# Attention stages of a two-model transformer kernel: three more engines in program order, and a new order of work

## The chip, the core and the metric

The kernel runs on one core of one Trainium2 chip. The core has five engines with instruction streams of their own: TensorE (PE in the profile; PEld is its weight load), VectorE (DVE), ScalarE (ACT), GpSimd (POOL) and SyncE (SP), which issues most DMA transfers. Engines meet through semaphores: an instruction waits on its engine until the instructions that it depends on are done, and what stands behind it on that engine waits too. The metric is the time of one execution on the device, in microseconds (us).

## The reference

Two stacks of two layers each run one after the other on one sequence of 256 tokens, model width 1024, in float32.

```python
# first stack, per layer
x = x + 0.5 * swiglu(rms_norm(x, norm_ffn1), w_ffn1_gate, w_ffn1_up, w_ffn1_down)   # hidden 2816
x = x + mixer(rms_norm(x, norm_mix))        # nsa (8 heads) beside moba (8 heads), then w_out
x = x + 0.5 * swiglu(rms_norm(x, norm_ffn2), ...)
# inside the nsa half of the mixer
kc = gelu(flat(k_cmp + pos_ck) @ w_ck1) @ w_ck2      # w_ck1: 2048 x 256; vc likewise with w_cv1
o = g0 * attend(q, kc, vc) + g1 * selected_blocks(rope(q), ...) + g2 * window(rope(q), ...)
# second stack, per layer (hybrid)
proj = rms_norm(x) @ w_in                   # aq ak av | index q k w | bq bk bv | gates
score = sum_h iw_h * relu(iq_h . ik);  keep the 64 best keys of each query
ya = attention(rope(norm(aq)), rope(norm(ak)), av) over the kept keys         # 8 heads
yb = (softmax(b1) - lam * softmax(b2)) @ bv, normed                           # 4 heads
x = x + (g_a * (ya @ w_up_a) + g_b * (yb @ w_up_b)) @ w_out
x = x + swiglu(rms_norm(x), ...)            # hidden 2816
```

## The kernel before

There are ten stages, in this order: feed-forward, mixer, feed-forward (twice, the first stack), then hybrid, feed-forward (twice, the second). All 256 tokens stay in SBUF, and every stage streams its weights from HBM. A weight chunk of 1 MB is loaded by SP into a buffer `raw` (three buffers of that name; a load waits until the chunk before it in its buffer has been used up). ACT copies the chunk into `hi` in TensorE's reduced float32 format (line 188), and DVE subtracts to get the rest, `lo` (line 189), each in two halves. PE then multiplies three times, with `hi` and `lo` (lines 209 to 211 for a projection). There are four buffers each of `hi` and `lo`.

In the attention stages, PE's own order is written out by hand (`tc.manual_schedule(engines={ENG.PE})`); the other engines' instructions are put in order by the scheduler of the framework. Work for PE comes in two kinds. A list of items, the class `Fill`, holds the large projections of the stage; each is a generator that yields after every few matmuls, and `fill.us(2.5)` runs the next matmuls of the list for about 2.5 us of PE's time, `fill.until("q")` runs the list until the item `q` is done. Between these calls stand the small steps that depend on other engines: transposes (`heads_T`, line 412), scores (line 430), the turning of the exponentials (`p_T`: `P` is transposed on PE and copied to `PT` by ACT, line 455, and DVE, line 458), values (line 486).

The weights of an item are asked for, and split, in one go when the item before it starts (`fetch(i + 1)`).

In the mixer, `blocks` turns the keys and values for the compression, `comp` multiplies them with `w_ck1` and `w_cv1` (line 788). These two matrices come in two halves of 1 MB each through the same `raw` buffers, unsplit: `ck`, `cv` for half 0, `ck'`, `cv'` for half 1. Behind them come a gelu (`z`), and a small product (line 819).

In the hybrid stage, `heads(name)` squares and sums a projection (ACT line 1020, DVE line 1023), takes the power -1/2 on POOL (`hr`, line 203) and applies the rope, `rope_full`: POOL multiplies with the cosine (line 966) and adds (line 976), DVE multiplies with the sine (lines 967 and 970) and with `hr` (line 981). The four projections `xa`, `xk` (sparse half) and `xb`, `xc` (difference half) go through this, then are transposed into `aqT`, `akT`, `bqT`, `bkT` (line 418 is DVE's copy). The index rope is all on DVE, makes `ix` and `ikd`; PE transposes these and DVE copies the result to `iT` (line 1081), from which line 1096 makes the index scores. The choice of the 64 best is 8 pairs of a maximum-of-eight and a replacement (lines 1123 and 1124) for each of two query blocks.

`pipeline` then runs over slots (12 in a mixer, 8 in a hybrid stage): at slot n it issues the scores of slot n + 1, fills, turns slot n, fills, multiplies slot n with its values, fills. `attend` makes such a slot; its coefficient multiplies `P` on DVE (line 471) and, for the last third, on POOL (line 472).

Of the kernel before, what the change touches and what calls it, by code (L numbers as in the profile page):

```python
# [16 lines left out]
ENG = mybir.EngineType  # L17
PSUM = bass.MemoryType.PSUM
# [3 lines left out]
D = 1024  # L22
# [4 lines left out]
NEG = -1e30  # L27
# [6 lines left out]
class K:  # L34
# [196 lines left out]
    def to_residual(self, yh, yl, w, nk, scale, after, held=2, fill=False):  # L231
# [27 lines left out]
        def fetch(c):  # L259
            src = w(c) if callable(w) else w[c * 256 : (c + 1) * 256, :].rearrange("(j p) n -> p j n", p=128)  # L260
            return self.weights(src, [2, D])
# [19 lines left out]
        if fill:  # L281
            return [(None, lambda c=c: fetch(c), lambda hl, c=c: run(c, hl), None) for c in range(nch)], end
        for c in range(nch):
            for _ in run(c, fetch(c)):
                pass
# [3 lines left out]
    def ffn(self, pr, wg, wu, wd, scale, after, start=None, load=None, extra=None):  # L289
# [3 lines left out]
        with tc.tile_pool(name="ffn", bufs=2) as fp:  # L293
# [33 lines left out]
            for c in range((NF + 3) // 4):  # L327
# [25 lines left out]
                if extra is not None and c == 2:  # L353
                    with tc.high_priority(150):
                        extra()
# [5 lines left out]
    def proj_item(self, name, w, c0, n, pr, done):  # L361


        def fetch():
            return [
                self.weights(
                    w[h * 512 : (h + 1) * 512, c0 : c0 + n].rearrange("(k p) f -> p k f", p=128), [4, n]
                )
                for h in range(2)
            ]  # L370
# [15 lines left out]
        return name, fetch, run, None  # L386
# [59 lines left out]
    def p_T(self, pool, p, n, k1):  # L446
# [9 lines left out]
        for i in range(n):  # L456
            nc.tensor.transpose(k1[:, 128 * i : 128 * i + 128], p[:, i, 128:256], self.ident)
        nc.vector.tensor_copy(pt[:, :, 256:384], k1[:, 0 : 128 * n].rearrange("p (i q) -> p i q", i=n))
        return pt

    def attend(self, pool, qk, vs, mask, coef, bank, end, start=True, stop=True):
# [5 lines left out]
        def scores():  # L467
            p, sm = self.scores_exp(pool, qk(), mask)
# [6 lines left out]
            st["p"] = p  # L475

        def turn():
            st["o"] = bank()

            st["pt"] = self.p_T(pool, st["p"], 2, st["o"][:, 256:512] if start else self.acc())  # L480
# [10 lines left out]
        return scores, turn, values  # L491

    def pipeline(self, fill, slots, post, a, b, c):


        slots[0][0]()
        fill.us(3.5)
        for n, (_, turn, values) in enumerate(slots):
            if n + 1 < len(slots):
                slots[n + 1][0]()  # L500
            fill.us(a)
            turn()
            fill.us(b)
            values()
            if n in post:
                post[n]()
            fill.us(c)
# [18 lines left out]
    def mixer(self, l, pr, after):  # L526
# [3 lines left out]
        with tc.tile_pool(name="mix", bufs=1) as mp, ExitStack() as es:  # L530
# [22 lines left out]
            es.enter_context(tc.manual_schedule(engines={ENG.PE}))  # L553
# [99 lines left out]
            def out_rows(c):  # L653
# [19 lines left out]

            rope2(kv[:, :, 256:384])
            next(blocks)
            fill.us(3.0)
# [4 lines left out]
            fill.us(4.0)  # L681
            next(comp)
            fill.us(1.5)
# [5 lines left out]
            fill.us(1.0)  # L689
# [8 lines left out]
            next(comp)  # L698
            fill.us(1.5)
            next(comp)  # L700
            next(comp)
            fill.us(1.0)
            next(comp)
            fill.us(1.2)
            self.heads_T(qrT, q, 0, self.psT, 0.125)
            fill.us(1.2)
            next(comp, None)
            fill.us(0.5)
            self.heads_T(qrT, q, 1, self.psO, 0.125)
            fill.us(0.3)  # L710
            probs = self.cmp_probs(mp, cp, qT, kcb, gt, tok)
            fill.us(1.5)
# [5 lines left out]
                1: lambda: self.heads_T(mq, tok["mq"], 0, self.psT, 0.125),  # L718
                2: lambda: self.heads_T(mq, tok["mq"], 1, self.psT, 0.125),
                5: lambda: self.heads_T(mk, tok["mk"], 0, self.psT),  # L720
                6: lambda: self.heads_T(mk, tok["mk"], 1, self.psT),
# [43 lines left out]
    def compress(self, mp, l, flats, kcb, vcb):  # L765
# [17 lines left out]
        for h in range(2):  # L783
            for i, w in enumerate(ws):
# [9 lines left out]
                if h == 0 and i == 1:  # L794
                    ws = fetch(1)
# [811 lines left out]
```

## Time and profile before

| what | us |
| --- | --- |
| median of 3 runs | 1923.4 (1920.32 to 1925.4) |
| the profiled execution: its time | 1922.36 |
| the profiled execution: its span | 1920.7 |
| PE busy (matmuls) | 1824.2, 95% of the span |
| DVE busy | 1312.5, 68% |
| ACT busy | 1000.1, 52% |
| POOL busy | 618.9, 32% |

The span runs from the first to the last instruction of the profile; the time has 1.7 us around it. All times of day below are microseconds from the span's start. A row of a timeline gives start, length, engine, line, operation, out<-in, and in brackets the idle time before it with what ended it. Matmuls are pipelined, so their lengths overlap.

### The profile page before, as it was taken

How to read it: one execution, taken by the hardware profiler on the slowest of the kernel's cores; microseconds unless marked ns; L12 is line 12 of the kernel's file. 1: busy time of each engine (PE TensorE's matmuls, PEld its weight loads, DVE VectorE, ACT ScalarE, POOL GpSimd, SP SyncE). 2: the span in 40 equal slices, each digit the busy share in tenths (PEclk: the TensorE clock that was granted, in tenths of full speed). 3: DMA queues.
4: the chain of work that ended last, by engine and by line, in shares of the span. 5: the costliest groups of instructions: out<-in, count | busy, mean ns of one | idle time of the engine just before them, and what ended most of it. 6: DMA issues, size and time to landing. Idle time of an engine off the chain costs nothing.

```text
span 1920.7 us, 27216 instructions
## 1 busy us (share of the span) xinstructions
PE 1824.2 (95%) x10136; PEld 1521.3 (79%) x10136; DVE 1312.5 (68%) x2170; ACT 1000.1 (52%) x1948; POOL 618.9 (32%) x660
## 2 busy tenths in 40 slices
PE   8899989999999999899999987899999897999999
PEld 7788866788788878667887776798888786888887
DVE  6766567776677665677766587767765787667763
ACT  6554445655555454456555544545554544546552
POOL 6451112254225411112542254012441442014540
PEclk9999999999999999999999998999999998999999
DMA  7547462354655464623546534245546444255543
GB/s 241 193 134 242 158 192 91 112 186 146 239 173 186 144 241 147 206 88 112 183 147 232 177 110 153 89 153 176 181 149 228 151 132 153 89 176 175 170 168 123
DMA packets 149077, 314.42 MB, mean 164 GB/s; under 512 B 5588, under 2 KB 30320, under 8 KB 148944
## 3 DMA queue, kind: packets, MB, share of 16 engines
q1 hardware_dynamic: 148016, 311.15, 49.4%
q0 software_dynamic: 896, 1.52, 0.4%
q8 instruction: 80, 1.31, 0.3%
q14 instruction: 53, 0.43, 0.1%
q10 hardware_dynamic: 32, 0.01, 0.0%
HBM read 311.61 MB, written 1.05 MB: 163 GB/s over the span
## 4 chain that ended last, share of the span: by engine, by line
PE 62%; DVE 17%; POOL 9%; ACT 7%; issue 4%; DMA 1%; SPq 0%; ACTq 0%; POOLq 0%; DVEq 0%
DVE lo L189 9%; PE acc L310 8%; PE acc L252 8%; PE acc L251 8%; PE acc L256 8%; PE acc L314 4%; PE acc L209 3%; PE psS L310 3%; ACT hi L188 3%; PE acc L210 3%; PE acc L211 3%; POOL hh L351 2%; POOL g L339 2%; ACT P L441 2%; PE psT L310 2%
## 5 line engine op out<-in xcount | busy, mean ns | idle before, releaser
L189 DVE TENSOR_TENSOR lo<-raw,hi 128x1024 fp32r<-128x1024 f32 (+1 forms) x604 | 745.3, 1258 | 206.7 <-ACT hi L188 202.3
L188 ACT ACTIVATE hi<-raw 128x1024 fp32r<-128x1024 f32 (+1 forms) x604 | 590.3, 1009 | 197.2 <-PE acc L256 110.8
L310 PE MATMUL acc<-xx,hi 128*128 128x512 f32 x1056 | 371.8, 397 | 8.0 <-DVE gcol L138 7.4
L314 PE MATMUL acc<-xx,lo 128*128 128x256 f32 x1056 | 291.4, 279 | 0.0
L310 PEld LDWEIGHTS acc<-xx,hi 128*128 128x128 f32 x1056 | 198.6, 189 | 53.0 <-DVE gcol L138 7.7
L252 PE MATMUL acc<-lo,gh 128*128 128x512 f32 x528 | 209.9, 397 | 3.8 <-DVE lo L189 3.8
L251 PE MATMUL acc<-hi,gh 128*128 128x512 f32 x528 | 209.4, 397 | 0.0
L314 PEld LDWEIGHTS acc<-xx,lo 128*128 128x128 f32 x1056 | 199.7, 189 | 1.8
L339 POOL TENSOR_TENSOR g<-g,rbc 128x256 f32<-128x256 f32 x132 | 136.4, 1046 | 175.1 <-DVE g L324 121.3
L310 PE MATMUL psS<-xx,hi 128*128 128x512 f32 x528 | 190.7, 395 | 2.1 <-ACT hi L188 2.1
L351 POOL TENSOR_TENSOR hh<-g,u 128x256 f32<-128x256 f32 x132 | 139.6, 1065 | 162.2 <-DVE u L324 162.2
L256 PE MATMUL acc<-hi,gl 128*128 128x512 f32 x528 | 173.7, 395 | 0.0
L209 PE MATMUL acc<-hi,xx 128*128 128x512 f32 (+2 forms) x416 | 171.2, 412 | 0.2 <-ACT xx L1462 0.2
L211 PE MATMUL acc<-hi,xx 128*128 128x512 f32 (+2 forms) x416 | 161.8, 389 | 1.1 <-DVE xx L1463 1.0
L210 PE MATMUL acc<-lo,xx 128*128 128x512 f32 (+2 forms) x416 | 161.5, 389 | 0.0
L349 POOL TENSOR_TENSOR g<-g,rbc 128x256 f32<-128x256 f32 x132 | 134.8, 1027 | 65.4 <-DVE g L342 65.4
L222 ACT ACTIVATE gh<-hh 128x256 fp32r<-128x256 f32 x132 | 55.2, 418 | 180.8 <-POOL hh L351 180.3
L314 PE MATMUL psS<-xx,lo 128*128 128x256 f32 x528 | 147.3, 279 | 1.1 <-DVE lo L189 1.1
L341 ACT ACTIVATE th<-g 128x256 f32<-128x256 f32 x132 | 55.0, 417 | 153.0 <-POOL g L339 152.6
L342 DVE SCALAR_TENSOR_TENSOR g<-th,g 128x256 f32<-128x256 f32 x132 | 83.4, 635 | 73.2 <-ACT th L341 73.2
L252 PEld LDWEIGHTS acc<-lo,gh 128*128 128x128 f32 x528 | 99.1, 188 | 28.6 <-DVE lo L189 5.4
L223 DVE TENSOR_TENSOR gl<-hh,gh 128x256 fp32r<-128x256 f32 x132 | 57.7, 437 | 92.2 <-ACT gh L222 92.2
(429 smaller groups left out, 3486.9 us busy)
## 6 DMA issues: line engine op xcount, KB each, us to landing
raw<-in_w_in_dram SPq DMA_DIRECT2D x60, 1024.0 KB, 5.1
raw<-in_w_ffn_down_dram SPq DMA_DIRECT2D x44, 1024.0 KB, 5.0
raw<-in_w_ffn_up_dram SPq DMA_DIRECT2D x40, 1024.0 KB, 5.1
raw<-in_w_ffn_in_dram SPq DMA_DIRECT2D x40, 1024.0 KB, 5.2
raw<-in_w_ffn_gate_dram SPq DMA_DIRECT2D x39, 1024.0 KB, 5.1
raw<-in_w_ffn_out_dram SPq DMA_DIRECT2D x22, 1024.0 KB, 5.0
raw<-in_w_out_dram SPq DMA_DIRECT2D x12, 1024.0 KB, 4.9
raw<-in_w_ffn_gate_dram SPq DMA_DIRECT2D x10, 512.0 KB, 3.8
```

The costliest lines, as they stand in the source:

```text
L188: nc.scalar.activation(hi[:, hs], raw[:, hs], AF.Copy),
L189: nc.vector.tensor_tensor(lo[:, hs], raw[:, hs], hi[:, hs].bitcast(F32), op=ALU.subtract),
L209: mm(out, ah, bh, start=start, stop=False)
L210: mm(out, ah, bl, start=False, stop=False)
L211: self.last = mm(out, al, bh, start=False, stop=stop)
L251: mm(accs[t, n], ah, hi[:, j, cs], start=k == 0, stop=False)
L252: mm(accs[t, n], ah, lo[:, j, cs], start=False, stop=False)
L256: mm(accs[t, n], al, hi[:, j, cs], start=False, stop=k == nk - 1)
L310: nc.tensor.matmul(banks[j], hi[:, k, fs], xk.rearrange("p u s -> p (u s)"), start=h == 0 and k == 0, stop=False,)
L314: self.last = nc.tensor.matmul(banks[j][:, 0:S], lo[:, k, fs], xk[:, 0, :], start=False, stop=h == 1 and k == 3,)
L339: nc.gpsimd.tensor_tensor(g, g, pr.rbc, op=ALU.mult)
L351: nc.gpsimd.tensor_tensor(hh, sgs[j], u, op=ALU.mult)
```

## The change

DVE, ACT and POOL are also taken out of the scheduler's hands inside the mixer and hybrid stages, so the order of their instructions there is now the order of the code. The code is laid out for it:

- The halves of a weight chunk are objects (`Chunk`): while an item of the list runs, the halves of the next item are split one by one, evenly over the item's steps. Before a half is split, the chunks of the next six halves (three chunks) are asked for, that is, their DMA is issued on SP. The list's first item is split before the stage's own code starts (`prime`).
- `fill.later(t, f)` puts a step off until `t` us of filled PE time have gone by. The rope's products, sum and norm, the squares' sums, and the top-k pairs (one each 1.5 us) are such steps.
- Hybrid: the items come in the order xb, xc, gate, xa, xk (before: xa, xk, gate, xb, xc); each pair of transposes moves along.
- `pipeline` keeps scores two slots ahead, and the coefficient's product is a step of its own (`weigh`) a fill later. The last third of `P` is multiplied on DVE instead of POOL.
- `comp`: `ck` and `cv` are taken in turn, so that both must have landed from its start; 16 matmul rows stand in one block where two blocks of 8 stood with fill between them.

```diff
+MANUAL = {ENG.PE, ENG.Activation, ENG.DVE, ENG.Pool}
...
-            es.enter_context(tc.manual_schedule(engines={ENG.PE}))
...
+            fill.prime()
+            es.enter_context(tc.manual_schedule(engines=MANUAL))
...
+class Chunk:
+    def ask(self):
+        if self.raw is None:
+            self.raw = self.k.wraw(self.src, self.shape)
+    def half(self, h):
...
+        nc.scalar.activation(self.hi[:, hs], self.raw[:, hs], AF.Copy)
+        nc.vector.tensor_tensor(self.lo[:, hs], self.raw[:, hs], self.hi[:, hs].bitcast(F32), op=ALU.subtract)
...
+    def split(self, upto):
+        while self.pos < min(upto, len(self.halves)):
+            for c, _ in self.halves[self.pos : self.pos + 6]:
+                c.ask()
+            c, h = self.halves[self.pos]
+            c.half(h)
+            self.pos += 1
...
+            if self.i + 1 < len(self.items):
+                a, b = self.upto[self.i + 1 : self.i + 3]
+                self.split(a + int((b - a) * min(1.0, self.n / steps)))
+            self.tick(t)
```

The compression and the mixer's calls around it:

```diff
         for h in range(2):
-            for i, w in enumerate(ws):
-                for j in range(0, 8, 2):
+            for j in range(0, 8, 2):
+                for i, w in enumerate(ws):
...
-                if h == 0 and i == 1:
-                    ws = fetch(1)
-                yield
+            if h == 0:
+                ws = fetch(1)
+            yield
...
             next(comp)
-            fill.us(4.0)
-            next(comp)
-            fill.us(1.5)
+            fill.us(4.5)
             next(comp)
             fill.until("q")
```

The slots, and the hybrid's rope and order:

```diff
-            nc.gpsimd.tensor_tensor(
+            nc.vector.tensor_tensor(
                 p[:, :, 256:384], p[:, :, 256:384], c[:, 2:4, None].to_broadcast([128, 2, 128]), op=ALU.mult
             )
...
+        for n in range(2):
+            slots[n][0]()
+            fill.tick(0.85)
+            fill.us(2.2)
+            slots[n][1]()
...
+            if n + 2 < len(slots):
+                slots[n + 2][0]()
...
+                    fill.later(3.2, root)
                     for t in range(2):
-                        self.rope_full(
+                        steps = self.rope_full(
...
+                        for d, f in zip(((1.2, 2.8, 6.8), (3.6, 5.2, 8.0))[t], steps):
+                            fill.later(d, f)
...
+            index_top(1.5)
             fill.until("xc")
-            fill.us(5.0)
+            fill.us(1.0)
             self.heads_T(bqT, tok["xb"], 0, self.psT, 0.125)
             self.heads_T(bqT, tok["xb"], 1, self.psO, 0.125)
-            fill.until("bv")
+            fill.until("g00")
             fill.us(2.0)
             self.heads_T(bkT, tok["xc"], 0, self.psT)
             self.heads_T(bkT, tok["xc"], 1, self.psO)
```

What this does to the order on two engines, at three places (lines are those of the file that a row is from; line 174 before is 175 after, 189 is 1578 in the attention stages, 981 is 1005, 1081 is 1115).

SP, the first mixer, before: `w_in` in chunks of 280 columns is item kw, those of 512 behind it are q, then (behind ck and cv) mq, and at the end mk and mv.

```order
L174 DMA raw<-in_w_in_dram 128x4x512 x2
L174 DMA raw<-in_w_in_dram 128x4x280 x2
L174 DMA raw<-in_w_in_dram 128x4x512 x2
L174 DMA raw<-in_w_ck_dram 128x8x256
L174 DMA raw<-in_w_cv_dram 128x8x256
L174 DMA raw<-in_w_in_dram 128x4x512 x2
L174 DMA raw<-in_w_ck_dram 128x8x256
L174 DMA raw<-in_w_cv_dram 128x8x256
L174 DMA raw<-in_w_in_dram 128x4x512 x4
```

SP, the same place, after:

```order
L175 DMA raw<-in_w_in_dram 128x4x512 x2
L175 DMA raw<-in_w_in_dram 128x4x280 x2
L175 DMA raw<-in_w_in_dram 128x4x512 x5
L175 DMA raw<-in_w_ck_dram 128x8x256
L175 DMA raw<-in_w_cv_dram 128x8x256
L175 DMA raw<-in_w_ck_dram 128x8x256
L175 DMA raw<-in_w_cv_dram 128x8x256
L175 DMA raw<-in_w_in_dram 128x4x512 x3
```

The first `ck` and `cv` stood in front of mq's two chunks; now they stand behind mq's two and the first of mk (the five are q, q, mq, mq, mk), and all four compression loads stand together.

DVE, the hybrid stage, before: the rope of xb and xc, its squares' sums (`ms`), and weight halves around it, up to the copy of `bqT`.

```order
L1023 TENSOR_REDUCE ms<-sq 128x8
L967 TENSOR_TENSOR t_10775<-xc,tab 128x8x32
L970 TENSOR_TENSOR t_10775<-xc,tab 128x8x32
L1023 TENSOR_REDUCE ms<-sq 128x8
L967 TENSOR_TENSOR t_10782<-xc,tab 128x8x32
L981 TENSOR_TENSOR xc<-t_10774,hr 128x512
L970 TENSOR_TENSOR t_10782<-xc,tab 128x8x32
L189 TENSOR_TENSOR lo<-raw,hi 128x1024
L981 TENSOR_TENSOR xc<-t_10781,hr 128x512
L189 TENSOR_TENSOR lo<-raw,hi 128x1024
L418 TENSOR_SCALAR bqT<-psO 128x4x128
```

DVE, the hybrid stage, after, from the first weight half behind the copy of `bqT` to the second norm of xc:

```order
L1578 TENSOR_TENSOR lo<-raw,hi 128x1024
L990 TENSOR_TENSOR t_10440<-xc,tab 128x8x32
L993 TENSOR_TENSOR t_10440<-xc,tab 128x8x32
L1162 MAX m_10511<-sc 128x8
L1163 MATCH_REPLACE sc<-m_10511,sc 128x256
L1578 TENSOR_TENSOR lo<-raw,hi 128x1024
L1162 MAX m_10531<-sc 128x8
L1163 MATCH_REPLACE sc<-m_10531,sc 128x256
L1005 TENSOR_TENSOR xc<-t_10437,hr 128x512
L1162 MAX m_10547<-sc 128x8
L1163 MATCH_REPLACE sc<-m_10547,sc 128x256
L1005 TENSOR_TENSOR xc<-t_10439,hr 128x512
```

The two norms of xc (`xc<-t,hr`) stood three and six rows behind the sums that `hr` is made from, with the other token half's product between them; now top-k pairs and weight halves stand there, and xc's rope comes after the copy of `bqT`, not in front of it.

DVE, the second hybrid stage, before: from the second `ikd` to the copy `iT`.

```order
L981 TENSOR_TENSOR ikd<-t_14043,hr 128x128
L967 TENSOR_TENSOR t_14164<-xa,tab 128x8x32
L970 TENSOR_TENSOR t_14164<-xa,tab 128x8x32
L1023 TENSOR_REDUCE ms<-sq 128x8
L967 TENSOR_TENSOR t_14171<-xa,tab 128x8x32
L981 TENSOR_TENSOR xa<-t_14163,hr 128x512
L970 TENSOR_TENSOR t_14171<-xa,tab 128x8x32
L1081 COPY iT<-psS 128x256
```

DVE, the same place, after:

```order
L989 TENSOR_TENSOR t_14111<-ix,tab 128x64
L990 TENSOR_TENSOR t_14112<-ix,tab 128x32
L993 TENSOR_TENSOR t_14112<-ix,tab 128x32
L998 TENSOR_TENSOR t_14111<-t_14111,t_14112 128x64
L1005 TENSOR_TENSOR ikd<-t_14111,hr 128x128
L1578 TENSOR_TENSOR lo<-raw,hi 128x1024 x2
L1115 COPY iT<-psS 128x256
```

The norm and the products of xa stood in front of the copy `iT`; now two weight halves stand there.

## Rows read from the trace of the kernel before

**Rows 1.** Windows by stage; the first line names the columns.

```profile
core 0: us, PE busy (x) PEld busy (x) DVE busy (x) ACT busy (x) POOL busy (x), PEclk, DMA share, GB/s
...
211.30:363.80 152.50, 142.34 (x837) 105.72 (x836) 100.33 (x220) 75.58 (x183) 26.48 (x43) 0.98 0.46 141
...
1082.70:1314.10 231.40, 205.17 (x1252) 176.06 (x1251) 166.85 (x308) 114.99 (x234) 65.61 (x62) 0.95 0.42 140
...
1504.30:1729.90 225.60, 203.17 (x1251) 174.53 (x1250) 163.50 (x304) 112.27 (x226) 66.29 (x56) 0.95 0.43 142
```

**Rows 2.** What PE waited for, first hybrid stage: us in total, times, longest.

```profile
PE psO L412 <- DVE bqT L418: 5.4, 1, 5.4
PE psO L486 <- ACT PT L455: 3.7, 1, 3.7
PE psS L1077 <- DVE ikd L981: 3.4, 1, 3.4
PE psT L412 <- DVE xc L981: 2.9, 1, 2.9
...
PE psS L430 <- DVE bkT L418: 1.9, 1, 1.9
PE psS L1074 <- DVE ix L974: 1.4, 1, 1.4
```

**Rows 3.** What PE waited for, second hybrid stage.

```profile
...
PE psS L1096 <- DVE iT L1081: 5.0, 1, 5.0
...
```

**Rows 4.** Timeline of DVE, first hybrid stage, around the norms of xc.

```profile
1180.62 0.69 DVE L981 TENSOR_TENSOR xc<-t,hr 128x512 f32<-128x512 f32 x1 [3.09 <-POOL hr L203]
...
1181.57 2.30 DVE L189 TENSOR_TENSOR lo<-raw,hi 128x1024 fp32r<-128x1024 f32 x1
1185.02 0.69 DVE L981 TENSOR_TENSOR xc<-t,hr 128x512 f32<-128x512 f32 x1 [1.15 <-POOL t L976]
```

**Rows 5.** Timeline of POOL, the same place.

```profile
1177.68 2.91 POOL L203 TENSOR_TENSOR hr<-hv,neghalf 128x16 f32<-128x16 f32 x1
1181.46 1.33 POOL L966 TENSOR_TENSOR t<-xc,tab 128x512 f32<-128x512 f32 x1 [0.87 <-DVE xc L981]
```

**Rows 6.** Windows behind that wait.

```profile
1186.00:1190.00 4.00, 2.50 (x8) 2.21 (x9) 4.00 (x5) 0.00 (x0) 0.00 (x0) 0.50 0.50 144
```

**Rows 7.** Windows from the index rope to the copy of bkT, first hybrid stage.

```profile
1099.40:1192.60 93.20, 77.13 (x381) 62.59 (x380) 73.74 (x142) 39.79 (x57) 46.70 (x40) 0.93 0.39 129
```

**Rows 8.** DVE by line, first mixer: busy, mean ns | idle before.

```profile
L223 DVE TENSOR_TENSOR ol<-psO,oh 128x256 fp32r<-128x256 f32 x8 | 3.3, 418 | 3.3 <-ACT oh L222 3.2
```

**Rows 9.** DMA issues of SP, first mixer.

```profile
214.35 0.37 SPq L174 DMA_DIRECT2D raw<-in_w_ck_dram  x1
222.51 0.37 SPq L174 DMA_DIRECT2D raw<-in_w_cv_dram  x1
```

**Rows 10.** Timeline of PE, first mixer: the compression.

```profile
228.18 0.60 PE L747 MATMUL psS<-ident,kd 128*128 128x128 f32 x4
...
232.84 1.92 PE L788 MATMUL psS<-raw,fl 128*32 128x256 f32 x16
```

**Rows 11.** Timeline of DVE, first mixer, ahead of the compression.

```profile
230.15 1.08 DVE L759 TENSOR_TENSOR fl<-k,posT 128x240 f32<-128x240 f32 x2 [0.46 <-ACT k L753]
232.66 2.36 DVE L189 TENSOR_TENSOR lo<-raw,hi 128x1024 fp32r<-128x1024 f32 x2 [1.43 <-ACT hi L188]
```

**Rows 12.** The same transfers: count, KB each, median us to landing.

```profile
raw<-in_w_in_dram SPq DMA_DIRECT2D x7, 1024.0 KB, 5.1
...
raw<-in_w_cv_dram SPq DMA_DIRECT2D x2, 1024.0 KB, 6.7
```

**Rows 13.** What PE waited for, first mixer.

```profile
PE psO L486 <- ACT PT L455: 4.4, 5, 2.0
PE psS L819 <- issue: 2.9, 1, 2.9
PE psT L453 <- POOL P L472: 2.5, 1, 2.5
```

More of the change, by code (lines that the diff above doesn't have):

```diff
@@ L281, in to_residual @@
         if fill:
-            return [(None, lambda c=c: fetch(c), lambda hl, c=c: run(c, hl), None) for c in range(nch)], end
+            return [
+                (None, [Chunk(self, rows(c), [2, D])], 16, lambda hl, c=c: run(c, hl[0]), None) for c in range(nch)
+            ], end
         for c in range(nch):
-            for _ in run(c, fetch(c)):
+            for _ in run(c, self.weights(rows(c), [2, D])):
                 pass
@@ L361, in proj_item @@
     def proj_item(self, name, w, c0, n, pr, done):
[L364 to L370, printed above, removed]
+        chunks = [
+            Chunk(self, w[h * 512 : (h + 1) * 512, c0 : c0 + n].rearrange("(k p) f -> p k f", p=128), [4, n])
+            for h in range(2)
+        ]
         def run(hl):
@@ L384, in run @@
             done(ps)
[L386 removed]
+        return name, chunks, 16, run, None
     def proj(self, w, c0, n, xh, xl):
@@ L1254, in vals @@
                         )
-                return scores, turn, vals
+                return scores, weigh, turn, vals
             def norm_y():
@@ L1266, in norm_y @@
                     )
+                for t in range(2):
+                    fill.later(5.0 + 3.0 * t, lambda t=t: scale(t))
             def y_T(t):
@@ L1508 @@
 class Fill:
     def __init__(self, items):
-        self.items, self.got = list(items), {}
-        self.i, self.gen, self.debt, self.past = 0, None, 0.0, set()
-    def fetch(self, i):
-        if i < len(self.items) and i not in self.got:
-            self.got[i] = self.items[i][1]()
+        self.items = list(items)
+        self.halves = [(c, h) for it in self.items for c in it[1] for h in range(2)]
+        self.upto = [0]
+        for it in self.items:
+            self.upto.append(self.upto[-1] + 2 * len(it[1]))
@@ L1520, in step, with tick @@
+    def tick(self, t):
+        self.now += t
+        while True:
+            due = sorted(x for x in self.tasks if x[0] <= self.now and x[2] is not None)
+            if not due:
+                return
+            self.tasks[due[0][1]] = (due[0][0], due[0][1], None)
+            due[0][2]()
     def step(self):
+        if self.i == len(self.items):
+            return False
+        name, chunks, steps, run, done = self.items[self.i]
         if self.gen is None:
-            if self.i == len(self.items):
-                return False
```

271 lines of the change are left out of this document (152 added, 119 removed).

## The prediction

> **What bounds the kernel now.** The page comes first: PE is busy for 95% of the span, so the kernel is bound by PE, and a change can gain only where PE stands still or runs slowly. The windows by stage say where that is. The reader is to see there that the first mixer has 142.3 us of PE work in 152.5, and the two hybrid stages 205.2 in 231.4 and 203.2 in 225.6, with a granted clock of 0.95 of full speed [rows 1]; the second mixer is like the first. In the feed-forward stages next to nothing is lost, and their orders are the same after the change, so the question is settled in four stages.
>
> The view of PE's waits names what is lost there. In the first hybrid stage PE waits 5.4 us for the copy `bqT`, 2.9 for the rope's norm of `xc`, 1.9 for `bkT`, 3.4 for `ikd`, 1.4 for `ix`, and 3.7 for the first turned slot of the sparse half, `PT` [rows 2]. In the second the same waits stand within 0.1 us, but for the index, where one wait of 5.0 us for `iT` takes the place of the two [rows 3]. All end at DVE or ACT, which have time to spare over the stage: DVE is busy for 166.9 of 231.4 us [rows 1]. So they are questions of order. The timeline shows one: DVE's norm of `xc` had waited 3.09 us for `hr`, a power of 2.91 us on POOL, and the second norm 1.15 us for POOL's sum [rows 4, 5]; the copy `bqT` stood behind both.
>
> [...]
>
> **The hybrid stages.** Six waits of the first add up to 5.4 + 2.9 + 1.9 + 3.4 + 1.4 + 3.7 = 18.7 us, in three places; with 3 x 1.3 for the clock, 22.6. In the second they are 5.4 + 2.9 + 1.9 + 5.0 + 3.7 = 18.9, with the clock 22.8. The order after takes what they wait for ahead of them. `xb` and `xc` are the first two items, and three further projections pass on PE before the sparse half is needed; the norms stand several rows behind their sums, with top-k pairs and weight halves in the time that POOL needs; `iT` has two weight halves ahead of it, not a norm that waits for POOL. For the sparse half's first slot, scores two slots ahead give ACT and DVE a slot more for the exponentials, coefficient and copy.
>
> What covers all that is DVE, and the cover is thin. From the index rope to `bkT`, before, DVE was busy 73.7 us and PE 77.1 in 93.2 us [rows 7], and the same five projections stand in this stretch after. Without waits PE passes it in about 79 us, so DVE is loaded to 73.7 / 79 = 93%. I leave 3 us in each stage for what comes late behind a DVE so full: the second norm of `xk` has only one weight half between it and the copy `akT`, and the first slot's scores have the evacuation of `akT` in front of their maxima. The gain is 22.6 - 3 and 22.8 - 3, together 39.4 us. Bounds: at best nothing is left (45 us), at worst only half of each wait goes (20 us).
>
> The product that moves from POOL to DVE costs DVE about what the 128x256 subtraction with two inputs takes, 0.42 us [rows 8]: 12 x 0.42 = 5.0 us in a mixer, 4 x 0.42 = 1.7 in a hybrid stage. A mixer's DVE is busy for 100.3 of 152.5 us [rows 1], which hides it. The other rewritings have the same instructions as before and cost nothing by themselves.
>
> **The mixers.** Here I expect a loss. The compression needs `ck` and `cv`. Before, SP issued them at 214.35 and 222.51 [rows 9], and PE began to multiply at 232.84 without a wait [rows 10]. After, SP's order has them behind mq's two chunks and the first of mk. There are three `raw` buffers, so each issue waits for the chunk three places ahead to be split up: `ck` for the last half of mq's first chunk, `cv` for the last half of mq's second. On DVE these halves stand directly behind `fl`, which ended at 230.15 + 1.08 = 231.2 before [rows 11] and has the same work in front of it. Four halves take twice the 2.36 us of a pair [rows 11], so the last cannot end before 236.0. It is later, since mq's second chunk is itself issued only when q's first is split, at about 229; it lands 5.1 to 6.7 us later [rows 12], at 234 to 236, and then ACT's and DVE's two halves follow, about 3.5 us. So `cv` is issued near 239, and lands 6.7 us later [rows 12], near 245.9. PE reaches the compression after 21 matmul rows of q where it was 18: these took from 228.18 to 232.84 [rows 10], 0.26 each, so at 233.6. It waits 245.9 - 233.6 = 12.3 us, with everything behind it on PE, and 1.3 for the clock. Bounds: 236.0 + 6.7 - 233.6 = 9.1, and 15 if the two loads share the bandwidth. The second halves are issued when the first are used up, near 250, land near 258, and are needed after the rest of q, at about 262: hidden.
>
> On the other side, the mixer's waits were 4.4 us for `PT`, 2.9 for the product of line 819, 2.5 for the first turn [rows 13]. Scores two slots ahead shorten the first; `z` still has a weight half in front of it on DVE, and the first turn still waits for a coefficient. I take 3.0 us back (bounds 0 and 9.8). A mixer loses 12.3 + 1.3 - 3.0 = 10.6 us; both, 21.2.
>
> **The sum.** 1922.4 (the profiled execution) - 39.4 + 21.2 = 1904.2; that execution is 1.0 us below the median of 1923.4, which changes nothing here. A measurement of this kernel tells about 0.3%, 5.8 us, from no change.
>
> **A rule to weigh.** The timeline has a weight half on DVE of 2.30 us, begun 0.1 us after POOL's product of 1.33 us [rows 4, 5], nearly twice the 1.18 of a half in a pair [rows 11]. So two such instructions do not overlap. The Trainium skill, page "SBUF — State Buffer", section "Who interferes with whom", says that a VectorE instruction with two SBUF inputs and a GpSimd instruction that reads SBUF exclude each other, and that the later one blocks for the whole of the first; this row agrees with it. By that, the sum would be larger by the rival "the port" below.
>
> **The rivals.**
> 1. *The port.* The rope's 16 POOL products and sums of a hybrid stage were partly beside an idle DVE; now DVE always has a half to run, and each of the 8 products may lengthen one by 2.30 - 1.18 = 1.1 us. DVE needs 73.7 + 9 = 82.7 us where PE needs 79: 3.7 us late in each stage, 1904.2 + 7.4 = 1911.6. For it, the rows; against it, the same pairs met before and are in the 73.7 already. Chance 0.10.
> 2. *In order, DVE waits for POOL (slower).* An instruction of DVE that waits for `hr` now holds all that stands behind it. If the delays of 6.8 and 8.0 us of PE's time are too short because POOL and DVE are behind, each of the four ropes costs DVE the 3.09 and 1.15 us of [rows 4]: 73.7 + 4 x 4.24 = 90.7 us against 79, so 11.7 us come back to each hybrid stage, with three slow spells, 3.9. The gain of a stage is then 22.7 - 3 - 15.6, about 4, and the time 1922.4 - 8 + 21.2 = 1935.6. It decides once DVE's own waits in that stretch pass 79 - 73.7 = 5 us. Against it: in the order the sums `ms` of `xc` stand eleven rows ahead of its first norm. Chance 0.17.
> 3. *No wait in the mixers.* If `ck` and `cv` land in time after all, mixers gain 3 each: 1922.4 - 39.4 - 6 = 1877. Against it, three buffers and SP's order. Chance 0.15.
> 4. *It doesn't do what it says.* The scheduler's order was near this one in its effects, waits only change names, and the mixers' loss is smaller: within 0.3% of before, 1922. Chance 0.10.
>
> **How the numbers follow.** The forecast has 0.48, with a range of its own from the bounds: 1904.2 - 6 - 10 to 1904.2 + 19 + 5 at the extremes, 1892 to 1918 for most of it. Faster by over 0.3%: 0.46 of the forecast, 0.15, and 0.08 of the port, 0.69. Slower by over 0.3%: most of rival 2, 0.17. The same: the rest, 0.14. The range of eight in ten reaches from 1880, which leaves out the lower half of rival 3, to 1934, which leaves out the upper half of rival 2.
>
> **What would show it.** In the profile after: a wait of PE for a transfer `raw` at the compression's line, 9 to 15 us in each mixer, SP's first `cv` issued near 239, not 222.5; mixer stages of about 163 us, and hybrid stages of about 211 and 206. The waits for `bqT`, `xc`, `iT` and `ikd` should be gone or under 1 us each, and the slow-clock spells of the hybrid stages with them. DVE's idle time ahead of the norms would show rival 2, weight halves over 2 us in the hybrid stages rival 1. The prediction is wrong if the compression starts without a wait, or if PE waits for DVE in the hybrid stages as long as before at other lines.

## The result, and the profile after

The changed kernel is slower: a median of 2022.3 us in 4 runs (2020.24 to 2026.66) against 1921.9 (1918.97 to 1925.4), a ratio of 1.0525 [1.0497, 1.0552]. The forecast was 1904.2 with a range up to 1934, so both its sign and its range were wrong. The span of the profiled execution grew from 1920.7 to 2025.0 us, and the mean granted clock fell from 0.983 to 0.960.

The windows of the first mixer, of its slots alone (from their first maximum `nm` to the end of the last one), and of the two hybrid stages, after (columns as in [rows 1]):

```profile
212.20:399.70 187.50, 149.12 (x832) 110.74 (x831) 97.14 (x227) 73.82 (x177) 15.66 (x31) 0.90 0.34 110
...
282.10:385.70 103.60, 81.17 (x442) 58.13 (x441) 53.78 (x144) 43.81 (x128) 4.89 (x8) 0.90 0.20 59
...
1158.70:1402.90 244.20, 212.52 (x1255) 180.97 (x1255) 168.72 (x311) 115.86 (x232) 58.02 (x58) 0.92 0.41 133
...
1594.50:1832.70 238.20, 209.22 (x1256) 179.44 (x1255) 165.80 (x308) 113.17 (x224) 58.84 (x53) 0.94 0.41 134
```

Against [rows 1] the mixer is 35.0 us longer (152.5 before) and the hybrid stages 12.8 and 12.6 (231.4 and 225.6). DVE and ACT are busy within 4 us of before in each of these; PE stands still more, and at 0.90 its matmuls are slower. To see where, I cut each of these stages at two points of the timelines: the first maximum `nm` of the slots, and the end of the last multiplication with the values (line 495, before 488). What lies ahead is the front, then the slots, then the tail.

| us | mixer: front, slots, tail | hybrid: front, slots, tail |
| --- | --- | --- |
| before | 58.8, 85.8, 7.8 | 111.2, 60.1, 60.1 |
| after | 69.9, 112.6, 4.9 | 99.8, 76.7, 67.6 |
| difference | +11.1, +26.8, -2.9 | -11.4, +16.6, +7.5 |

These are the first mixer and the first hybrid stage; in the second ones the differences are +10.6, +26.6, -2.9 and -11.7, +16.4, +7.8. The feed-forward stages add 9.8 us in all. So the slots alone cost 26.8 + 26.6 + 16.6 + 16.4 = 86.4 us, and they are a place that the forecast counted as a gain.

What PE waited for most after, first mixer (us in total, times, longest), which answers to [rows 13]:

```profile
PE psO L493 <- DVE PT L458: 16.1, 6, 4.9
PE psS L807 <- DMA raw<-in_w_ck_dram: 9.2, 1, 9.2
PE psS L807 <- DMA raw<-in_w_cv_dram: 2.9, 1, 2.9
```

The first rows of the same view of the first hybrid stage, which answers to [rows 2]:

```profile
PE psO L1283 <- DVE PT L458: 10.6, 4, 4.7
PE psO L493 <- DVE PT L458: 5.1, 3, 2.6
PE psS L1130 <- ACT iT L1114: 2.6, 1, 2.6
PE psO L410 <- DVE xa L1005: 2.2, 1, 2.2
PE psO L410 <- DVE xk L1005: 2.2, 1, 2.2
PE acc L252 <- ACT hi L1577: 2.1, 1, 2.1
PE psT L410 <- DVE xa L1005: 1.6, 1, 1.6
PE psS L1111 <- DVE ikd L1005: 1.2, 1, 1.2
```

The waits for `bqT`, `xc` and `bkT` are gone, as forecast, and `ck` and `cv` are waited for, as forecast. The large new name is `PT`, DVE's copy of the turned exponentials. The timeline of DVE in one mixer slot after shows what stands in front of it:

```profile
330.26 0.42 DVE L436 TENSOR_REDUCE nm<-psS 128x1 f32<-128x256 f32 x1
331.38 0.62 DVE L436 TENSOR_REDUCE nm<-psS 128x1 f32<-128x128 f32 x2 [0.69 <-ACT P L439]
332.65 0.29 DVE L436 TENSOR_REDUCE nm<-psS 128x1 f32<-128x128 f32 x1 [0.65 <-ACT P L439]
334.41 1.23 DVE L1578 TENSOR_TENSOR lo<-raw,hi 128x1024 fp32r<-128x1024 f32 x1 [1.47 <-ACT hi L1577]
335.55 0.16 DVE L635 TENSOR_SCALAR c<-sm 128x4 f32<-128x4 f32 x1
...
336.69 0.42 DVE L479 TENSOR_TENSOR P<-P,c 128x256 f32<-128x256 f32 x1
337.02 0.42 DVE L458 COPY PT<-psO 128x256 f32<-128x256 f32 x1
```

ACT in the same slot:

```profile
332.97 0.37 ACT L439 ACTIVATE P<-psS,nm 128x128 f32<-128x128 f32 x1 [0.36 <-DVE nm L436]
...
333.33 1.04 ACT L1577 ACTIVATE hi<-raw 128x1024 fp32r<-128x1024 f32 x1
```

And PE:

```profile
331.31 0.38 PE L457 MATMUL psO<-ident,P 128*128 128x128 f32 x2
...
337.59 0.65 PE L493 MATMUL psO<-PT,kv 128*64 128x256 f32 x4 [4.50 <-DVE PT L458]
```

The turned block stood ready in PSUM at 331.31 + 0.38 = 331.7. Its copy takes 0.42 us, but in written order it stands behind the scores of the next slot: four maxima, two for each head, of which DVE begins the second of a head only when ACT is done with the exponential of the first; a weight half, for which DVE waits 1.47 us, since ACT's `hi` stands behind the last exponential; and the coefficient and products. So it begins at 337.02, 5.3 us late, and PE waits 4.50. The Trainium skill, page "PSUM — Partial Sum Buffer", section "Engine vs sequencer instructions", says that the queues of ScalarE, VectorE and GpSimdE are strictly first in, first out; the trace agrees: DVE stood idle for 0.65 + 1.47 = 2.12 us of these 5.3, with the copy ready.

DVE in one slot of the first mixer before, where the scheduler had ordered it:

```profile
307.25 0.76 DVE L438 TENSOR_REDUCE nm<-psS 128x1 f32<-128x256 f32 x2 [0.62 <-PE psS L434]
308.36 0.29 DVE L438 TENSOR_REDUCE nm<-psS 128x1 f32<-128x128 f32 x1 [0.36 <-ACT P L441]
308.82 0.29 DVE L438 TENSOR_REDUCE nm<-psS 128x1 f32<-128x128 f32 x1 [0.17 <-ACT P L441]
309.39 0.42 DVE L458 COPY PT<-psO 128x256 f32<-128x256 f32 x1 [0.28 <-PE psO L457]
309.73 0.16 DVE L614 TENSOR_SCALAR c<-sm 128x4 f32<-128x4 f32 x1
```

There the heads took turns, no weight half stood among these rows, and the copy came ahead of the coefficient; it began when PE had turned the block.

The DMA issues of SP in the first mixer after, which answer to [rows 9]:

```profile
238.06 0.37 SPq L175 DMA_DIRECT2D raw<-in_w_ck_dram  x1
240.33 0.37 SPq L175 DMA_DIRECT2D raw<-in_w_cv_dram  x1
```

`ck` is issued 23.7 us later than before, `cv` 17.8. PE reaches the compression and waits for both:

```profile
243.76 1.07 PE L807 MATMUL psS<-raw,fl 128*32 128x256 f32 x4 [9.25 <-DMA raw<-in_w_ck_dram]
```

### The profile page after: what moved, and what is told of

Same layout as the page of the kernel before. It is cut to its first block, busy times and chain, and to the rows that moved or that the text cites. A ratio compares the mean times of both kernels' runs of the same rounds, so it can differ in the third digit from the quotient of the medians.

```text
span 2025.0 us, 27057 instructions
## 1 busy us (share of the span) xinstructions
PE 1863.4 (92%) x10136; PEld 1547.9 (76%) x10136; DVE 1318.4 (65%) x2202; ACT 1003.2 (50%) x1948; POOL 577.3 (29%) x628
## 3 DMA queue, kind: packets, MB, share of 16 engines
q8 instruction: 79, 1.29, 0.3%
## 4 chain that ended last, share of the span: by engine, by line
PE 65%; DVE 15%; ACT 9%; POOL 5%; issue 5%; DMA 2%; ACTq 0%; POOLq 0%; DVEq 0%
PE acc L312 10%; PE acc L253 7%; PE acc L257 7%; PE acc L252 7%; PE acc L316 5%; PE psS L312 5%; DVE lo L1578 4%; ACT P L439 3%; PE acc L210 3%; PE psT L312 2%; PE acc L212 2%; DVE lo L190 2%; PE acc L211 2%; PE psS L316 2%; PE psO L312 2%
## 5 line engine op out<-in xcount | busy, mean ns | idle before, releaser
L190 DVE TENSOR_TENSOR lo<-raw,hi 128x1024 fp32r<-128x1024 f32 (+2 forms) x436 | 535.3, 1254 | 158.6 <-ACT hi L189 153.7
L189 ACT ACTIVATE hi<-raw 128x1024 fp32r<-128x1024 f32 (+2 forms) x436 | 423.4, 999 | 150.0 <-PE acc L257 107.5
L312 PE MATMUL acc<-xx,hi 128*128 128x512 f32 x1056 | 376.8, 401 | 9.8 <-DVE gcol L139 7.4
L312 PEld LDWEIGHTS acc<-xx,hi 128*128 128x128 f32 x1056 | 199.6, 190 | 58.5 <-DVE gcol L139 7.7
L1578 DVE TENSOR_TENSOR lo<-raw,hi 128x1024 fp32r<-128x1024 f32 (+1 forms) x168 | 204.3, 1229 | 47.4 <-ACT hi L1577 47.2
L1577 ACT ACTIVATE hi<-raw 128x1024 fp32r<-128x1024 f32 (+1 forms) x168 | 167.4, 1035 | 4.4 <-PE acc L212 4.2
L344 DVE SCALAR_TENSOR_TENSOR g<-th,g 128x256 f32<-128x256 f32 x132 | 82.4, 628 | 74.9 <-ACT th L343 74.9
```

The lines of the kernel that those rows point to most:

```text
L189: nc.scalar.activation(hi[:, hs], raw[:, hs], AF.Copy),
L190: nc.vector.tensor_tensor(lo[:, hs], raw[:, hs], hi[:, hs].bitcast(F32), op=ALU.subtract),
L312: nc.tensor.matmul(banks[j], hi[:, k, fs], xk.rearrange("p u s -> p (u s)"), start=h == 0 and k == 0, stop=False,)
L1577: nc.scalar.activation(self.hi[:, hs], self.raw[:, hs], AF.Copy)
L1578: nc.vector.tensor_tensor(self.lo[:, hs], self.raw[:, hs], self.hi[:, hs].bitcast(F32), op=ALU.subtract)
```

## The experiments

The first theory after the result: in the slots, the written order of DVE and ACT makes PE wait for `PT`, and `ck` and `cv` cost the rest. Its main rival: scores two slots ahead with two buffers `P`, and the third product on DVE, are too much for a slot, whoever orders the other engines. In the table, the phases of the first mixer and the first hybrid stage are cut as above.

| kernel | us | ratio to before | mixer: front, slots, tail | hybrid: front, slots, tail |
| --- | --- | --- | --- | --- |
| e1_pe_only | 1903.0 | 0.9887 [0.9866, 0.9908] | 57.7, 83.4, 6.6 | 107.1, 57.9, 60.7 |
| e2_heads | 1984.1 | 1.0314 [1.0297, 1.0330] | 71.4, 100.8, 4.9 | 100.4, 68.2, 67.9 |
| e3_ck_early | 2002.7 | 1.0405 [1.0380, 1.0429] | 60.2, 112.0, 4.9 | 98.9, 76.7, 66.7 |
| e4_weigh_late | 1997.8 | 1.0382 [1.0363, 1.0402] | 68.8, 99.2, 6.8 | 98.9, 77.1, 66.7 |
| e5_before_inorder | 2166.4 | 1.1271 [1.1248, 1.1295] | 81.8, 129.2, 7.9 | 143.5, 82.2, 63.0 |
| e6_pe_only_ck | 1896.8 | 0.9854 [0.9834, 0.9875] | 53.3, 82.2, 6.5 | 107.1, 56.7, 60.7 |
| e7_dve_free | 1953.8 | 1.0154 [1.0137, 1.0171] | 64.5, 94.2, 6.7 | 104.2, 62.1, 65.7 |
| e8_act_free | 1993.7 | 1.0363 [1.0346, 1.0379] | 68.1, 108.0, 6.0 | 94.9, 72.0, 66.6 |
| e9_front | 1905.7 | 0.9913 [0.9891, 0.9935] | 71.5, 82.6, 6.6 | 99.3, 55.3, 60.7 |
| e10_best | 1878.6 | 0.9778 [0.9751, 0.9805] | 53.2, 82.2, 6.6 | 101.1, 56.9, 60.8 |
| e11_order_mended | 1946.5 | 1.0128 [1.0111, 1.0145] | 58.5, 90.4, 4.8 | 98.0, 69.5, 67.8 |
| e12_pool_product | 2024.0 | 1.0538 [1.0518, 1.0558] | 69.0, 109.8, 5.6 | 98.0, 76.4, 66.7 |

**e1_pe_only.** The changed code, with PE alone in written order.

```diff
-MANUAL = {ENG.PE, ENG.Activation, ENG.DVE, ENG.Pool}
+MANUAL = {ENG.PE}
```

> Only PE keeps its written order in the mixer and hybrid stages; DVE, ACT and POOL go back to the scheduler, with all the rest of the change in place. Theory 1 (the written order of DVE and ACT puts the copies PT behind the next slot's maxima, exponentials, weight half and coefficient): PE's waits for PT, 16.1 us in the first mixer and 15.7 in the first hybrid stage of the changed kernel, fall below 6 each, and with the clock the time falls from 2022 by 50 us or more, to 1940 to 1975; the wait for ck and cv, 9.2 and 2.9 us, stays, since it comes from SP's order. Theory 2 (scores two slots ahead with two buffers P, and the third product on DVE, are too much for the slot whatever the order): the waits for PT stay above 10 us a stage and the time above 2000.

Measured 1903.0, below what either theory expected: it is even 1.1% faster than before. PE's order is the changed one here, and the third product is on DVE, so the rival falls: 2022.3 - 1903.0 = 119 us are the net price of the written order of the other three engines. DVE in one slot of this kernel:

```profile
320.11 0.75 DVE L436 TENSOR_REDUCE nm<-psS 128x1 f32<-128x256 f32 x2
320.77 1.22 DVE L1578 TENSOR_TENSOR lo<-raw,hi 128x1024 fp32r<-128x1024 f32 x1
321.90 0.48 DVE L436 TENSOR_REDUCE nm<-psS 128x1 f32<-128x128 f32 x2
322.30 0.41 DVE L458 COPY PT<-psO 128x256 f32<-128x256 f32 x1
323.06 0.17 DVE L635 TENSOR_SCALAR c<-sm 128x4 f32<-128x4 f32 x1 [0.34 <-ACT P L439]
```

The scheduler takes the wide maxima of both heads one behind the other and then both narrow ones, so that ACT has an exponential to run while DVE takes the next maximum, and it puts the copy ahead of the coefficient. The same window of the slots shows what that does to PE:

```profile
268.90:346.10 77.20, 72.81 (x449) 53.41 (x449) 59.08 (x155) 45.10 (x131) 8.30 (x12) 1.00 0.34 100
```

The same slots took 103.6 us after. PE's busy time is 72.8 us here, at a clock of 1.00, and was 81.2 at 0.90: of the 26.4 us, 8.4 are longer matmuls, with the lower clock, and 18.0 standstill.

**e2_heads.** Still in written order, with the maxima of both heads taken in turn.

```diff
-        for i, b in enumerate(ps):
-            for t, c0, c1 in ((0, 0, 256), (1, 256, 384)):
+        for t, c0, c1 in ((0, 0, 256), (1, 256, 384)):
+            for i, b in enumerate(ps):
```

> The changed kernel with one thing else: in the scores of a slot, both wide maxima and exponentials come first and then both narrow ones (the two loops are exchanged), so that the two heads take turns. In the written order each of four maxima waits for the exponential in front of it: 302.1 to 305.2, 3.2 us, where the kernel before took 307.25 to 309.6, about 2.4. Theory 1: the chain of a slot gets 0.7 to 0.9 us shorter and all of it comes back at the copies PT: 40 slots, most of which wait, 20 to 32 us with the clock, 1990 to 2002. Rival (the weight halves and the coefficient in front of the copies decide, the chain is hidden): under 8 us, above 2014.

Measured 1984.1: 38 us less than the changed kernel, more than expected. The expectation has each of the four maxima wait for an exponential; the rows above show that two of the four do (0.69 and 0.65 us). With the heads in turn DVE and ACT overlap: maxima and exponentials of one such slot took 2.3 us here (324.84 to 327.10), 3.1 after. The slots lose 11.8 us of their 26.8 in the mixer and 8.5 of 16.6 in the hybrid stage.

**e3_ck_early.** `ck` and `cv` are asked for before the stage's own code, ahead of mq's chunks.

```diff
-            for c, _ in self.halves[self.pos : self.pos + 6]:
+            for c, _ in self.halves[self.pos : self.pos + self.ahead]:
...
-            fill.prime()
+            fill.prime(5)
             es.enter_context(tc.manual_schedule(engines=MANUAL))
+            next(comp)
...
-            next(comp)
```

> The changed kernel with the first ck and cv asked for in front of mq's chunks, as before the change, and nothing else. If the order of SP's queue is the whole cause of the wait at the compression, the 9.2 + 2.9 us of each mixer go, with 1.3 us for the clock: 24 to 30 us, 1992 to 1998, and no longer wait of PE elsewhere. If the compression waits for something else as well, fl or the split of q: 10 to 15 us are left and the time is above 2008.

Measured 2002.7, between the two expectations. `ck` was issued at 215.87 and `cv` at 230.08 in the first mixer. The front of the mixers falls by 9.7 us each, of the 11.1 and 10.6 that it had grown, which bears the cause out; the waits that stay there are 2.2 us for `cv` and 0.8 for `fl`.

**e4_weigh_late.** The coefficient and products of slot n + 2 behind the copies `PT` of slot n + 1.

```diff
+        late = None
...
+            if late and not rest:
+                late()
+                late = None
...
+                if late:
+                    late()
+                    late = None
...
-                slots[n + 2][1]()
+                late = slots[n + 2][1]
```

> The changed kernel with the coefficient of slot n + 2 (the reciprocal and the products on P) put behind the copies PT of slot n + 1 on DVE, where it stood in front of them. The coefficient takes 1.6 us (295.5 to 297.05). Theory 1: the copy on DVE comes 1.6 us earlier in each of the 36 slots that have a coefficient in front, of which PE feels some 1.0 to 1.6: 30 to 55 us, 1967 to 1992. Rival (ACT's copy behind the exponentials is as late as DVE's, so that moving DVE's gains little): ACT's copy ends 2.5 us ahead of DVE's at the slot at 294.8, so at most this; under 15 us if it is otherwise late, above 2007.

Measured 1997.8, 24.5 us less, and less than expected. In the mixer the slots lose 13.4 us; in the hybrid stage nothing. There the wait changes its name, as PE's longest waits in its first hybrid stage show:

```profile
PE psO L493 <- DVE c L1188: 6.4, 3, 4.1
PE psO L1290 <- DVE PT L458: 4.4, 1, 4.4
PE psO L1290 <- DVE c L1188: 3.0, 2, 2.2
```

The coefficient now comes late itself: one place in a written order is bought with another.

**e5_before_inorder.** The code of before, with all four engines in written order.

```diff
-            es.enter_context(tc.manual_schedule(engines={ENG.PE}))
+            es.enter_context(tc.manual_schedule(engines={ENG.PE, ENG.Activation, ENG.DVE, ENG.Pool}))
```

> The kernel before, with nothing changed but that DVE, ACT and POOL also keep the order of the code in the mixer and hybrid stages. Theory 1: that order has a next item's four weight halves, the whole rope and the whole top-k in one lump, and in each slot the next slot's four maxima, exponentials and coefficient in front of the copies PT; 40 slots at 3 to 4 us, and waits at every rope: 2100 to 2250, slower than the changed kernel, whose rewriting then gives back a part. Rival (the written order is harmless with the old code, and the new code, two slots ahead, is what costs): below 2000.

Measured 2166.4, as expected. So the change has two parts of opposite sign: written order costs 244.5 us on the old code, and the new layout of the code takes back 144 of them. With PE alone in written order the new layout is a gain of 19 us (1903.0 in e1 against 1921.9).

**e6_pe_only_ck.** e1 with the edit of e3.

> PE alone in written order, as in the run e1, and the first ck and cv asked for ahead of mq's chunks, as in e3. In e1 PE still waits 4.0 and 1.5 us for cv and ck in a mixer. If these waits come from SP's order alone they go: 2 x 5.5, and 1 to 3 for the clock, 1889 to 1893. If the scheduler's order already made up for them elsewhere, the time stays within 4 us of e1, 1903.

Measured 1896.8, 6.2 below e1 and some 4 us above the first range; the mixers are 142.1 and 142.8 us long, 5.6 and 3.2 less than in e1. So the late `ck` and `cv` cost less where the scheduler orders DVE, ACT and POOL, but they cost there too.

**e7_dve_free** and **e8_act_free.** The changed kernel, with DVE or ACT given back to the scheduler.

```diff
-MANUAL = {ENG.PE, ENG.Activation, ENG.DVE, ENG.Pool}
+MANUAL = {ENG.PE, ENG.Activation, ENG.Pool}      # e7
+MANUAL = {ENG.PE, ENG.DVE, ENG.Pool}             # e8
```

> The changed kernel with DVE given back to the scheduler; PE, ACT and POOL keep the written order. Theory 1 says which engine's order costs: the copy PT that ends last is DVE's in most slots (at 297.4, ACT's at 294.8), so that most of the loss comes back: 60 to 90 us of the 119 between the changed kernel and e1, 1932 to 1962. Rival (ACT's written order, four exponentials and a weight half ahead of its copy, is as bad by itself): less than 40 us come back, above 1982.

> The changed kernel with ACT given back to the scheduler; PE, DVE and POOL keep the written order. Theory 1: DVE's copy stays behind the chain and the coefficient, so little comes back, 10 to 30 us, 1992 to 2012. Rival (the two chains are one, and ACT's order is what makes the maxima wait): 60 us or more, below 1962.

Measured 1953.8 and 1993.7, both as expected: 68.5 us come back with DVE's order, 28.6 with ACT's, 119 only with all three engines'. In e7 the wait is still there under the other engine's name, in the first mixer:

```profile
PE psO L493 <- ACT PT L453: 5.9, 6, 1.8
```

**e9_front.** Four engines in written order up to the slots, PE alone from there on.

```diff
-            es.enter_context(tc.manual_schedule(engines=MANUAL))
+            ms = es.enter_context(ExitStack())
+            ms.enter_context(tc.manual_schedule(engines=MANUAL))
...
+            ms.close()
+            ms.enter_context(tc.manual_schedule(engines={ENG.PE}))
             self.pipeline(fill, slots, {3: norm_y}, 1.3, 1.3, 1.3)
```

The same lines stand in the mixer.

> The four engines keep the written order up to the start of the slots, and from there on only PE does. Theory 1 (the written order is good for the rope, the top-k and the transposes, and bad in the slots): the first hybrid stage loses its waits for PT, 15.7 us, and keeps the short waits in front of the slots, so it is shorter than e1's 225.8, by 0 to 6 us; mixers keep the wait for ck and cv of 12 us, so they are 5 to 9 us longer than e1's 147.7. Time 1903 + 14 - 6, about 1905 to 1920. Rival (the written order costs in front as well, at the norms of xa and xk and the index): hybrid stages longer than e1's by 3 us or more, above 1920.

Measured 1905.7, as expected in sum, by two misses of opposite sign: the first hybrid stage is 10.4 us shorter than in e1 where 0 to 6 were expected, the first mixer 12.9 longer where 5 to 9 were. This is near the kernel that the forecast described: the hybrid stages are 215.4 and 211.0 us long (forecast: about 211 and 206), the mixers 160.6 and 161.5 (forecast: about 163). That the median lies 1.5 us from the forecast's 1904.2 is in part luck: the hybrid stages are 4 to 5 us longer than forecast and the mixers about 2 shorter, and these lengths come from the slowest of the four runs, of 1912.5 us. The slots and the tail are back at 82.6 and 55.3, 6.6 and 60.7.

**e10_best.** From each part the better order: mixers with PE alone in order and the edit of e3, hybrid stages as in e9.

> Put together from what the runs gave: mixers with PE alone in written order and ck and cv early (e6), hybrid stages with four engines in written order up to the slots and PE alone from there (e9). If the stages do not depend on each other, the hybrid stages take 215.4 and 211.0 us in place of 224.5 and 219.7: 1896.8 - 17.8 = 1879, 1874 to 1885. If the gain of e9's front is lost again (its weight halves come due in the slots), above 1890.

Measured 1878.6 (1875.09 to 1884.28), as expected; 2.2% faster than before, and the fastest of all. Its mixers are 142.0 and 145.5 us long, its hybrid stages 218.8 and 210.6.

**e11_order_mended.** The edits of e2, e3 and e4 together, all engines in written order.

> All four engines in written order throughout, with the code's order mended at the three places: the heads take turns in the scores (e2), ck and cv early (e3), the coefficient behind the copies PT (e4). If the three add up: 2022 - 38 - 20 - 24 = 1940. The first and the last shorten the same wait, so less is likely, 1940 to 1965. Theory 1 says that a written order is no loss by itself, so it can come near the scheduler's 1903; rival (only the scheduler's freedom to take what is ready helps): above 1975.

Measured 1946.5, as expected: 75.8 us come back, where the three alone gave 38.2 + 19.7 + 24.5 = 82.4. The mixer is near before (153.7 us), the hybrid's slots (69.5) and tail (67.8) are not. It stays 43.5 us above e1: most of this lies in the slots and the tail of the hybrid stages and in the mixers' slots (90.4, 83.4 in e1), and which rows of the written order cost it was not tested.

**e12_pool_product.** The last third of `P` on POOL again.

```diff
-            nc.vector.tensor_tensor(
+            nc.gpsimd.tensor_tensor(
                 p[:, :, 256:384], p[:, :, 256:384], c[:, 2:4, None].to_broadcast([128, 2, 128]), op=ALU.mult
```

> The changed kernel with the last third of P multiplied on POOL again. On DVE the third product takes 0.42 us behind two of 0.35; on POOL it took 0.72 beside them. If DVE's chain sets the slot, each of 32 slots gains 0.2 to 0.4 us: 6 to 14 us, 2008 to 2016. If the product's place does not matter, or the two engines' products stretch each other (in the kernel before two products on DVE beside POOL's took 0.87 and 0.70 instead of 0.35): within 4 us of 2022, or above.

Measured 2024.0: no effect, so the rival of that run holds. Moving the 0.42 us of DVE in the slot's chain to POOL gives nothing.

## Why the prediction was wrong

**The step that failed** is the term for the slots: "Scores two slots ahead shorten the first [...] I take 3.0 us back (bounds 0 and 9.8)" in the mixers, and for the hybrid stages "scores two slots ahead give ACT and DVE a slot more". Measured are +26.8 and +26.6 in the mixers' slots, +16.6 and +16.4 in the hybrids', where I had -3.0 and -5.0 (`PT` 3.7 and the clock 1.3). That is 59.4 + 43.0 = 102.4 of the 122.5 us between the forecast change of -18.2 and the measured +104.3 of the spans. The step counted when the scores could be issued, not what they then stand in front of: on DVE and ACT, the scores of slot n + 2 are written ahead of the copies of slot n + 1. The bounds were wrong with it. They reached from no effect to a full gain, as if the scheduler still put the copy where it was needed; a loss was not bounded at all, though taking the scheduler away from three engines is the change's first line. The prediction's own sign of being wrong came: PE waits for DVE in the first hybrid stage as long as before at other lines, 10.6 + 5.1 = 15.7 us at the copies `PT`. The order's rows of DVE and ACT in one slot, with the durations of a maximum, an exponential, a half and the products behind them, are where this could have been read ahead of the result; the prediction looked at the order at three other places only.

**The clock.** The sums of the prediction add 1.3 us for the clock to each long wait. No run shows this as the price of a wait: [rows 6] show one window at a granted clock of 0.50 with PE busy for 2.50 us. What the runs show is a whole stretch: in the first mixer's slots after, at 0.90, PE was busy 8.4 us longer than in e1, at 1.00.

**Rival 2** named the mechanism (an instruction that waits holds what stands behind it), but at the ropes. There it hardly happened; DVE at the norms of `xc` and `xk` that waited, first hybrid stage after:

```profile
1211.94 0.69 DVE L1005 TENSOR_TENSOR xc<-t,hr 128x512 f32<-128x512 f32 x1 [0.33 <-POOL t L998]
...
1252.06 1.77 DVE L1005 TENSOR_TENSOR xk<-t,hr 128x512 f32<-128x512 f32 x1 [1.64 <-POOL hr L204]
```

DVE waited 0.3 us ahead of the norms of `xc` and 1.6 ahead of those of `xk`, where [rows 4] have 3.09 and 1.15 for one pair. It happened in the slots, and also in the tail of the hybrid stages (+7.5 and +7.8), which I took as unchanged. ACT there, after:

```profile
1369.39 0.63 ACT L223 ACTIVATE mh<-ma 128x512 fp32r<-128x512 f32 x1 [3.32 <-POOL ma L1344]
1369.93 1.05 ACT L1577 ACTIVATE hi<-raw 128x1024 fp32r<-128x1024 f32 x1
...
1374.29 0.63 ACT L223 ACTIVATE mh<-ma 128x512 fp32r<-128x512 f32 x1 [3.31 <-POOL ma L1344]
1374.83 1.04 ACT L1577 ACTIVATE hi<-raw 128x1024 fp32r<-128x1024 f32 x1
```

Each weight half stands behind an `mh` that waits 3.3 us for POOL's sum, so a half comes every 4.9 us where ACT needs 1.04 for one, and PE waits for `hi` (2.1 us, above). ACT's order is not the only one that costs here: in e8, with ACT given back, the tail is still 66.6. There DVE's halves stand behind an `ml` that waits for `mh`:

```profile
1351.17 0.69 DVE L224 TENSOR_TENSOR ml<-ma,mh 128x512 fp32r<-128x512 f32 x1 [2.13 <-ACT mh L223]
1351.78 1.22 DVE L1578 TENSOR_TENSOR lo<-raw,hi 128x1024 fp32r<-128x1024 f32 x1
```

PE waits 2.5 and 1.3 us for such halves in that tail. With all three engines given back (e1, e9) the tail is 60.7.

**The mixers' front** was right in mechanism and size. `cv` was issued at 240.33 (forecast: near 239), PE reached the compression at 243.76 - 9.25 = 234.5 (233.6) and waited 9.2 + 2.9 = 12.1 us (12.3). With the clock I had 13.6; the front grew by 11.1 and 10.6, and e3 took 9.7 of each back.

**The hybrids' front** was right in kind and too large in size. The waits for `bqT`, `xc` and `bkT` went; in the index, 3.4 + 1.4 us became 1.2 + 2.6 in the first stage, and the 5.0 for `iT` became 0.9 in the second; but `xa` and `xk` came up with 2.2 + 2.2 + 1.6 = 6.0 us, where I left 3 for what comes late. Without the 5.0 us that I counted for `PT`, the forecast for the front was -14.6 and -14.8; measured are -11.4 and -11.7. Not all of this is the written order: with PE alone in order (e1) the first front is 107.1, so of the 11.4 us 4.1 came with the new layout of the code. With the slots free of written order, e9 shows both terms together: 16.0 + 14.6 = 30.6 us of the 39.4, and its slots are 4.8 us shorter than before, as the term of `PT` had it.

**The product on DVE** was costed at nothing behind other work; e12 agrees, though DVE's order was on PE's path.

**Rival 1, the port.** Single instructions lengthen: the first norm of `xc` took 1.45 us beside POOL's product of 1.29, the second 0.69. But ahead of the slots the 27 halves of the hybrid stage have a mean of 1.319 us, against 1.311 for 31 before, so the halves lose no more than before. The first norms of `xa` and `xk` took 1.57 and 1.77 us (0.69 before); whether that is part of the 6.0 us that PE waits for them, no run shows. **Rival 3** (1877, no mixer wait) needed what the change doesn't do; e10, with `ck` early and the slots given back, stands at 1878.6, but by another way: the mixers' other three engines are in the scheduler's order there. **Rival 4** is excluded by the result. The feed-forward stages' 9.8 us, most of them in the stages behind the mixers (+2.9 each), I had at nothing; in e9 these are +0.9 and +0.8, so they hang on the order in the slots and behind them, which was not followed further.

## What to carry to other kernels

When an engine is taken out of the scheduler's hands, price its order at the loop that repeats most often, not at the places for which the change is written: list what stands ahead of each instruction that PE waits for, with every wait for another engine, and set the sum against PE's work in one round. Scores further ahead were no gain while they were written ahead of the copies of the slot that is due; written behind them they were not tested. And written order needn't hold for a whole stage: on the code laid out for it, it gains 7.3 us in the front of the first hybrid stage (99.8 against 107.1 in e1) and loses 18.8 in its slots, and the fastest kernel here changes over between the two. On the old code it loses in that front too: 143.5 against 111.2.

## What the runs showed of the hardware

- When a maximum on DVE and an exponential on ACT alternate, each engine's idle time is the other's instruction and little else: ACT sat idle for 0.36 us ahead of an exponential, 0.29 of them the maximum that it needs; the maximum ended at 332.65 + 0.29 = 332.94 and the exponential began at 332.97. DVE sat idle for 0.69 and 0.65 us ahead of the second maximum of each head, while ACT ran the exponential of the first. Four pairs, two for each head in turn, occupy 330.26 to 333.34, 3.1 us; with the heads alternating they took 2.3, and the exchange of two loops (e2) was worth 38 us of the kernel.
- The clock takes part in such a loss. In the mixer's slots waits of up to 4.9 us came with a granted clock of 0.90, where the same work without them ran at 1.00: about a third of the loss in these slots (8.4 of 26.4 us) is longer matmuls, not waiting.
